# Elementwise work of a hybrid decoder layer divided anew between ScalarE and VectorE

## The chip, the core and the metric

The kernel runs on one core of a Trainium2 chip. The metric is the device time of one execution in microseconds (us). The kernel before takes 871.72 us, the median of three runs (871.52 to 871.88). A profile of one execution shows, per instruction, when it ran on TensorE (PE, its weight loads apart as PEld), VectorE (DVE), ScalarE (ACT), GpSimd (POOL) and in the DMA queues of SyncE (SP).

## The reference

One layer: x is RMS-normed and multiplied with w_in (2048 rows) into the inputs of three groups. Their outputs, each times a SiLU gate, are joined, multiplied with w_out, added to x, and normed again. SEQ is 512, D_MODEL 2048, everything float32.

```python
h = rmsnorm(x, norm_g[l]);  proj = h @ w_in[l]
u = cv_a * jax.nn.sigmoid(cv_b)
u = causal_depthwise_conv(u, conv_w[l], conv_b[l])            # 31 taps, 512 channels
u = jax.nn.silu(layernorm(u, conv_ln_g[l], conv_ln_b[l]))
y_conv = (u @ w_conv_pw[l]) * jax.nn.silu(cv_gate)
logf = jax.nn.log_sigmoid(f_logit + b_f[l])                   # forgetting attention, 8 heads of 128
s = einsum(q, k) * Dh ** -0.5;  s = where(mask, s + c[t] - c[s], -inf);  p = softmax(s)
y_fox = (p @ v) * jax.nn.silu(fox_gate)
mk, mv = split(rmsnorm(mem, mem_norm_g[l]) @ w_mem_kv[l])     # 256 memory tokens, 4 heads
y_mem = memory_attention(mq, mk, mv) * jax.nn.silu(mem_gate)
x = x + concatenate([y_conv, y_fox, y_mem]) @ w_out[l];  return rmsnorm(x, final_g)
```

## The kernel before

Every float32 operand of a product is cut into two rounded parts, hi + lo: ScalarE casts the hi part (line 93, or line 96 with a scale), VectorE subtracts it from the source for the lo part (line 94, or 97). Three products, hi by hi, lo by hi and hi by lo, add up in one PSUM bank (lines 104 to 106 where it is plain, line 732 in the heads, line 981 in the output). Weights come as raw tiles of 128 x 1024 by DMA (six buffers), and become `whi` and `wlo`, which have three buffers each: the cast of a tile waits until TensorE is through with the tile three before it. Of PSUM, five banks circulate under the tag `pj` and three under `at`.

The stages follow each other in time: memory values and keys (to about 62 us; line 104 with the names `mh`, `ml`); x rows (line 212 multiplies each of four 128 x 2048 tiles by its 1/rms, in place) and their transposes by TensorE into `pj` and `at` banks, from which ScalarE makes `hh` and VectorE `hl` (`x_column`, line 262; some columns' transposes run between the products of the last memory key, `pj_689` in the orders below); the first projections by `hh` and `hl` from 66 us; the convolution's inputs with 31 taps each on VectorE and the memory attention; the gates; from about 343 to 690 us the eight forgetting heads; then the output product to 860.8 us, and an end of 8.0 us without TensorE.

A head's two features (queries with keys, values with gate) are made by Winograd's form of Strassen's seven products (`pair`, line 713). Its first product goes to the bank x1, is copied by ScalarE into SBUF as p1 (line 707) and added by VectorE to the third product's bank x2 (line 700). The softmax (`probs`) takes four query blocks of 128, 256, 384 and 512 keys: logits plus bias (line 803), negated maximum (line 805), Exp with a sum (line 807), reciprocal (line 808) and division (line 809). `gate_values` (line 777) makes SiLU from Sigmoid on ScalarE and a product on VectorE. Sigmoid and Exp need different activation tables, so table loads stand on ScalarE.

What an engine runs next is set at build time: the scheduler plans a timeline with its own costs and lays down one fixed order for each engine. An engine waits at the first instruction that isn't ready, whatever is ready behind it. So a change of the elementwise work can change the order of everything near it.

Of the kernel before, what the change touches and what calls it, by code (L numbers as in the profile page):

```python
# [47 lines left out]
def hybrid_layer_kernel(  # L48
# [41 lines left out]
    def split(hi, lo, src, scale=None):  # L90
        """hi + lo == src (times scale): twelve significant bits each."""
        if scale is None:
            ins = nc.scalar.copy(hi, src)  # L93
            nc.vector.tensor_tensor(lo, src, hi.bitcast(F32), ALU.subtract)  # L94
        else:
            ins = nc.scalar.activation(hi, src, AF.Identity, scale=scale)
            nc.vector.scalar_tensor_tensor(
                lo, src, scale, hi.bitcast(F32), ALU.mult, ALU.subtract
            )
        return ins.ins  # L100
# [16 lines left out]
    def operand(src, out=None):  # L117
        """src [P, n, c], whole -> its two parts."""
        if out is None:
            out = tuple(  # L120
                wp.tile(list(src.shape), F32R, tag=t, name=nm(t), bufs=3) for t in ("whi", "wlo")
            )
        split(*out, src)
        return out

    def weights(src, n, c, raw=None, hold=None):
        """src [n * P, c] -> k -> (hi, lo) of its k-th P rows."""
        half = n // 2
        src = src.rearrange("(k p) f -> p k f", p=P)
        parts = []  # L130
        for j in range(2):
            rows = slice(j * half, (j + 1) * half)
            r = raw_tile(half, c) if raw is None else raw[:, rows, :]
            nc.sync.dma_start(out=r, in_=src[:, rows, :])
            parts.append(operand(r, tuple(t[:, rows, :] for t in hold) if hold else None))
        return lambda k: tuple(t[:, k % half, :] for t in parts[k // half])

# [1 line left out]
    ident = const.tile([P, P], F32, name="ident")  # L139
# [11 lines left out]
    ht = ctx.enter_context(tc.tile_pool(name="ht", bufs=1, side="right", reuse_waits="tile"))  # L151
    # x normed, [feature, token], two features' tiles in each
    hs_ = [
# [10 lines left out]

    # ---- start: memory values and keys (rows transposed as they come, their
    # norm applied to the results), x normed and transposed ----
    with tc.tile_pool(name="start", bufs=1) as st:
# [40 lines left out]
        def norm_x(t):  # L208
            rs = st.tile([P, 1], F32, tag="rs", name=nm("rs"), bufs=4)
            sum_squares(rs, xrows[t])  # L210
            rstd(rs)
            nc.vector.tensor_scalar(xrows[t], xrows[t], rs, None, ALU.mult)

# [83 lines left out]
    def project(f0, per=0):  # L297
        """[P features from f0, tokens] in PSUM."""
        w = weights(w_in[:, f0 : f0 + P], KT, P)
# [6 lines left out]
    def silu_of(pool, o, tag, bufs):  # L306
        """silu of a PSUM tile."""
        sg = pool.tile([P, S], F32, tag=tag, name=nm(tag), bufs=bufs)
        nc.scalar.activation(sg, o, AF.Sigmoid)
        nc.vector.tensor_tensor(sg, o, sg, ALU.mult)  # L310
        return sg

# [1 line left out]
    NC = CW // P  # L314
    PAD = TAPS - 1
    with tc.tile_pool(name="conv", bufs=1, reuse_waits="tile") as cp:
# [3 lines left out]
        def taps_of(c, up):  # L320
            a = acc[c]

            def first():
                nc.vector.tensor_scalar(
                    a, up[:, 0:S], cwt[:, c, 0:1], conv_b_c(c), ALU.mult, ALU.add
                )
# [26 lines left out]
        def mem_probs(ma, h, q):  # L353
            qh, ql = q
            pr = []
            for i2 in range(2):
# [15 lines left out]
                for j in range(2):  # L372
                    nc.vector.tensor_scalar(pp[:, j, :], pp[:, j, :], sm[:, j : j + 1], None, ALU.mult)
                pr.append(pp)
# [77 lines left out]
        def forget_columns():  # L452
            c = fgs["c"]
            pc = at((P, NT * NH))
            for i in range(NT):
                nc.tensor.transpose(
                    pc[:, i * NH : (i + 1) * NH], c[:, i * P : (i + 1) * P], ident[:NH, :NH]
                )
            nc.vector.tensor_copy(ccol.rearrange("p i h -> p (i h)"), pc)
        conv_in(0)  # L460
# [7 lines left out]
        with tc.tile_pool(name="matt", bufs=1, reuse_waits="tile") as ma:  # L468
            # the channel norm's sums and the gates run between the heads
            gates = []  # L470
# [26 lines left out]
            def normalise():  # L497
# [15 lines left out]
                for c in range(NC):  # L513
                    a = acc[c]
                    sg = spare()
                    nc.scalar.activation(sg, a, AF.Sigmoid, bias=ln_b_c(c), scale=ln_g_c(c))
                    nc.vector.tensor_scalar(a, a, ln_g_c(c), ln_b_c(c), ALU.mult, ALU.add)
                    nc.vector.tensor_tensor(a, a, sg, ALU.mult)
                    split(*cs[c], a)
# [17 lines left out]

        # sums of h's quarters (token halves by feature halves); the last takes
        # the place of the quarter that no product needs
        spool = ctx.enter_context(  # L540
# [55 lines left out]

    # ---- the output projection's operands; what they need of the room of h and
    # its sums falls free with the last pair's products. The convolution's and
    # the memory's parts of y are multiplied as they are; the heads' parts by the
    # same form as the pairs, with sums of their quarters (token halves by halves  # L600
    # of the heads) ----
    NB = D // S
# [55 lines left out]
    def head_ys(j, fa, fb):  # L658
        """Heads j and 4 + j, whole: their quarters' parts and those of the
        sums, which take the room of fa and fb."""  # L660
        base = [room_h(w, j, (2, S)) for w in "hl"]
# [23 lines left out]

# [1 line left out]
    with tc.tile_pool(name="fox", bufs=1, reuse_waits="tile") as fx:  # L687
# [22 lines left out]
        def pair(fa, fb):  # L710
            """Features fa.. and fb.., P each, by Winograd's form of Strassen's
            seven products: the first in PSUM, by token halves, the second in
            SBUF. In three steps, for another pair's to come between."""
            HK = KT // 2
# [8 lines left out]

            # Sums are taken in PSUM: a product adds onto what its bank holds,
            # which copies and an addition have read or changed before. Only a
            # bank's first product starts afresh.
            def product(o, w, a, start=False):
# [12 lines left out]
            yield  # L740
            p1 = kept(x1, "p1")
            less(b11, b12, b11)
            product(zo, b11, s1, start=True)
            p5 = kept(zo, "p5")
            less(b11, b22, b11)
            product(x2, b11, s2, start=True)
            plus(x2, x2, p1)
            u2 = kept(x2, "u2")
# [18 lines left out]
        def queries_keys(xs, col):  # L767
            q, k = parts("fq"), parts("fk")
            split(*k, col)
            for x_, hi, lo in zip(xs, halves(q[0]), halves(q[1])):  # L770
                split(hi, lo, x_)
            return q, k

        def gate_values(xs, col):
            gate = fx.tile([P, S], F32, tag="fgate", name=nm("fgate"), bufs=2)
            for x_, g in zip(xs, halves(gate)):
                nc.scalar.activation(g, x_, AF.Sigmoid)
                nc.vector.tensor_tensor(g, x_, g, ALU.mult)
            vp = at()
# [7 lines left out]
        def probs(h, q, k):  # L787
# [3 lines left out]
            for i in range(NT):  # L791
                n = (i + 1) * P
                sl = slice(i * P, n)
                b = fx.tile([P, n], F32, tag=f"b{i}", name=nm("b"))
                nc.scalar.activation(b, cb[:, :n], AF.Identity, scale=-1.0, bias=ccol[:, i, h : h + 1])  # L795
                nc.gpsimd.affine_select(  # L796
                    out=b[:, sl], in_=b[:, sl], pattern=[[-1, P]], compare_op=ALU.is_ge,
                    fill=MASKED, base=0, channel_multiplier=1,
                )
                w = max(n, M)  # L800
                sp = at((P, w))
                mm3(sp, (q[0][:, sl], q[1][:, sl]), (k[0][:, :w], k[1][:, :w]), True, True)
                nc.vector.scalar_tensor_tensor(b, sp[:, :n], SC, b, ALU.mult, ALU.add)
                ng = fx.tile([P, 1], F32, tag="ng", name=nm("ng"), bufs=4)
                nc.vector.tensor_reduce(ng, b, AX.X, ALU.max, negate=True)
                sm = fx.tile([P, 1], F32, tag="sm", name=nm("sm"), bufs=4)
                nc.scalar.activation(b, b, AF.Exp, bias=ng, accum_out=sm)
                nc.vector.reciprocal(sm, sm)
                nc.vector.tensor_scalar(b, b, sm, None, ALU.mult)
                res.append(b)  # L810
# [76 lines left out]

# [1 line left out]
    head_ys(3, heads[6], last_y)  # L889
    with tc.tile_pool(name="outp", bufs=1, reuse_waits="tile") as op:  # L890
# [3 lines left out]
        gb = op.tile([P, D], F32, name="gb")  # L894
        # by token halves and column blocks
        res = [[op.tile([P, 2, S], F32, name=f"res{h}{n}") for n in range(NB)] for h in range(2)]
# [22 lines left out]
        def sides(n):  # L919
            """y's other parts; the last time, a token tile at a time and to the end."""  # L920
            final = n == NB - 1
# [19 lines left out]
            for t in range(NT):  # L941
                if not final:
                    add(of(t, n), os_[t])
                    continue
                # the very last one by halves, for less to follow its products
                spans = [ALL] if t < NT - 1 else [slice(0, M), slice(M, S)]
# [133 lines left out]
```

## Time and profile before

| | |
|---|---|
| median of three runs | 871.72 us (871.52 to 871.88) |
| span of the profiled execution | 868.8 us, 14045 instructions |
| around the span | 2.9 us (871.72 less 868.8; the page has no other time of that execution) |
| TensorE busy | 855.3 us, 98% |
| VectorE busy | 704.8 us, 81% |
| ScalarE busy | 436.2 us, 50% |
| chain that ended last | PE 95%, ACT, DVE, DMA and issue 1% each |

The chain is followed back from the last instruction to whatever released each step; it says that TensorE's own work makes up the span, and that there is little waiting to remove. In the timeline view a row has its start, its duration, engine, line, operation, output and inputs (without buffer numbers), its count where several are joined, and in brackets the idle time before it with its releaser. Records of matmuls overlap: a product on 256 columns is 0.28 us long, and the next one starts 0.12 us after it.

### The profile page before, as it was taken

What the parts mean: (1) busy time and instruction counts of PE and PEld (TensorE: products, weight loads), DVE (VectorE), ACT (ScalarE), POOL (GpSimd) and SP (SyncE); (2) the same over time, 40 slices, a digit from 0 to 9 for tenths busy, and PEclk for the clock granted to TensorE, in tenths of its full rate; (3) what the DMA queues carried; (4) which work ended last, traced back from release to release, by engine and by line L of the source; (5) the groups of instructions that cost most, each with busy time, mean ns of one, the idle gap of its engine ahead of it and who ended that gap; (6) DMA issues with size and microseconds to landing.
All of it is one profiled execution on the core that took longest, in us unless ns stands there. A gap on an engine that the chain in (4) does not pass through costs nothing.

```text
span 868.8 us, 14045 instructions
## 1 busy us (share of the span) xinstructions
PE 855.3 (98%) x5562; PEld 775.1 (89%) x5562; DVE 704.8 (81%) x1051; ACT 436.2 (50%) x679; POOL 45.1 (5%) x76
## 2 busy tenths in 40 slices
PE   8999999999999999999999999999999999999996
PEld 6897887888888888999999999999999888998995
DVE  4686799999977998998787878878797886876964
ACT  4874322224346544566565555656464852443523
POOL 1011000000000002010101010101010000000001
PEclk9999999999999999999999999999999999999999
DMA  9972233333332333233434243333334627351415
GB/s 323 356 197 76 70 82 105 97 97 89 94 85 85 109 90 117 79 106 109 121 93 127 74 120 101 107 103 91 107 84 146 239 73 267 97 195 49 146 49 194
DMA packets 143265, 107.52 MB, mean 124 GB/s; under 512 B 3892, under 2 KB 126816, under 8 KB 142560
## 3 DMA queue, kind: packets, MB, share of 16 engines
q1 hardware_dynamic: 141696, 102.52, 39.3%
q0 software_dynamic: 1504, 4.11, 1.3%
q8 instruction: 43, 0.70, 0.3%
q14 instruction: 22, 0.18, 0.1%
HBM read 98.46 MB, written 8.14 MB: 123 GB/s over the span
## 4 chain that ended last, share of the span: by engine, by line
PE 95%; issue 1%; ACT 1%; DVE 1%; DMA 1%; SPq 0%; POOL 0%; POOLq 0%; ACTq 0%
PE pj L732 33%; PE pj L104 13%; PE pj L105 13%; PE pj L106 13%; PE pj L981 8%; PE at L104 3%; PE at L105 3%; PE at L106 3%; PE at L820 1%; DMA raw<-in_w_mem_kv_dram 1%; PE pj L409 0%; PE pj L408 0%; PE pj L262 0%; PE at L262 0%; PE at L782 0%
## 5 line engine op out<-in xcount | busy, mean ns | idle before, releaser
L93 ACT CAST whi<-raw 128x1024 fp32r<-128x1024 f32 x205 | 215.1, 1051 | 324.2 <-PE pj L105 110.9
L94 DVE TENSOR_TENSOR wlo<-raw,whi 128x1024 fp32r<-128x1024 f32 x205 | 250.1, 1221 | 87.5 <-ACT whi L93 86.6
L105 PE MATMUL pj<-hl,whi 128*128 128x512 f32 x352 | 139.6, 397 | 0.0
L106 PE MATMUL pj<-hh,wlo 128*128 128x512 f32 x352 | 139.1, 396 | 0.0
L104 PE MATMUL pj<-hh,whi 128*128 128x512 f32 x352 | 138.9, 396 | 0.0
L732 PE MATMUL pj<-hh,wlo 128*128 128x256 f32 x480 | 135.0, 281 | 0.0
L732 PE MATMUL pj<-hl,whi 128*128 128x256 f32 x480 | 134.9, 281 | 0.0
L732 PE MATMUL pj<-hh,whi 128*128 128x256 f32 x480 | 134.8, 281 | 0.0
L703 DVE TENSOR_TENSOR raw<-raw,raw 128x1024 f32<-128x1024 f32 x76 | 92.7, 1220 | 0.5
L732 PEld LDWEIGHTS pj<-hl,whi 128*128 128x128 f32 x480 | 90.4, 188 | 0.1
L732 PEld LDWEIGHTS pj<-hh,whi 128*128 128x128 f32 x480 | 90.5, 188 | 0.0
L732 PEld LDWEIGHTS pj<-hh,wlo 128*128 128x128 f32 x480 | 90.4, 188 | 0.0
L329 DVE SCALAR_TENSOR_TENSOR acc<-up,cwt,acc 128x512 f32<-128x512 f32 x120 | 85.2, 741 | 0.4
L981 PE MATMUL pj<-whi,rh 128*128 128x256 f32 x448 | 80.0, 280 | 0.7 <-DVE sst L1035 0.4
L104 PEld LDWEIGHTS pj<-hh,whi 128*128 128x128 f32 x352 | 66.1, 188 | 15.9 <-PE pj L262 0.2
L106 PEld LDWEIGHTS pj<-hh,wlo 128*128 128x128 f32 x352 | 66.1, 188 | 15.7
L105 PEld LDWEIGHTS pj<-hl,whi 128*128 128x128 f32 x352 | 66.1, 188 | 15.5
L981 PEld LDWEIGHTS pj<-whi,rh 128*128 128x128 f32 x448 | 68.8, 188 | 1.3 <-DVE res L907 1.1
L981 PE MATMUL pj<-wlo,rh 128*128 128x256 f32 x224 | 62.3, 279 | 0.0
L981 PEld LDWEIGHTS pj<-wlo,rh 128*128 128x128 f32 x224 | 42.1, 188 | 0.2
L796 POOL TENSOR_SCALAR_AFFINE_SELECT b<-b 128x128 f32<-128x128 f32 x32 | 21.3, 676 | 265.6 <-ACT b L795 234.0
L732 PE MATMUL pj<-s0h,whi 128*128 128x256 f32 x120 | 34.9, 291 | 0.0
(302 smaller groups left out, 1720.5 us busy)
## 6 DMA issues: line engine op xcount, KB each, us to landing
raw<-in_w_in_dram SPq DMA_DIRECT2D x104, 512.0 KB, 3.6
raw<-in_w_out_dram SPq DMA_DIRECT2D x32, 512.0 KB, 4.5
raw<-in_w_mem_kv_dram SPq DMA_DIRECT2D x12, 512.0 KB, 7.3
xr<-in_x_dram SPq DMA_DIRECT2D x4, 1024.0 KB, 7.8
res<-in_x_dram SPq DMA_DIRECT2D x8, 512.0 KB, 6.8
out_dram<-res SPq DMA_DIRECT2D x16, 256.0 KB, 2.8
rs<-yd SPq DMA_DIRECT2D x15, 256.0 KB, 4.6
mr<-in_mem_dram SPq DMA_DIRECT2D x8, 256.0 KB, 7.2
```

The source lines that it names most:

```text
L93: ins = nc.scalar.copy(hi, src)
L94: nc.vector.tensor_tensor(lo, src, hi.bitcast(F32), ALU.subtract)
L104: nc.tensor.matmul(o, ah, bh, start=start, stop=False)
L105: nc.tensor.matmul(o, ah, bl, start=False, stop=False)
L106: nc.tensor.matmul(o, al, bh, start=False, stop=stop)
L329: return lambda: nc.vector.scalar_tensor_tensor(a, up[:, j : j + S], cwt[:, c, j : j + 1], a, ALU.mult, ALU.add)
L703: nc.vector.tensor_tensor(o, p, q, ALU.subtract)
L732: nc.tensor.matmul(o, p[:, k, :], q, start=start and k == 0 and i == 0, stop=k == HK - 1 and i == 2, skip_group_check=True,)
L796: nc.gpsimd.affine_select(out=b[:, sl], in_=b[:, sl], pattern=[[-1, P]], compare_op=ALU.is_ge, fill=MASKED, base=0, channel_multiplier=1,)
L820: nc.tensor.transpose(tp[:, (i - j) * P : (i - j + 1) * P], pr[i][:, j * P : (j + 1) * P], ident)
L981: nc.tensor.matmul(o[:, m, :], p, q[:, k, :], start=start and k + m + i == 0, stop=k == HK - 1 and i == 2, skip_group_check=True,)
```

## The change

Six things change. The four row norms of x (line 212) go from VectorE to ScalarE. SiLU is one ScalarE activation instead of a Sigmoid and a VectorE product, in the gates and behind the convolution's norm. The first tap of each convolution channel block and the division of the probabilities, of memory and of forgetting heads, go to ScalarE. The logits with their bias and their maximum are taken in one fused VectorE instruction (`tensor_tensor_reduce`, with signs turned and the scale put into the queries' split). Strassen's first product is copied by ScalarE from bank x1 into bank x2, onto which the third product then adds, so p1 and its VectorE addition go.

```diff
--- before
+++ after
@@ -209,7 +209,7 @@
             sum_squares(rs, xrows[t])
             rstd(rs)
-            nc.vector.tensor_scalar(xrows[t], xrows[t], rs, None, ALU.mult)
+            nc.scalar.mul(xrows[t], xrows[t], rs)
         QC = D // 4
@@ -304,13 +304,12 @@
     def silu_of(pool, o, tag, bufs):
         sg = pool.tile([P, S], F32, tag=tag, name=nm(tag), bufs=bufs)
-        nc.scalar.activation(sg, o, AF.Sigmoid)
-        nc.vector.tensor_tensor(sg, o, sg, ALU.mult)
+        nc.scalar.activation(sg, o, AF.Silu)
         return sg
@@ -321,8 +320,8 @@
             a = acc[c]
             def first():
-                nc.vector.tensor_scalar(
-                    a, up[:, 0:S], cwt[:, c, 0:1], conv_b_c(c), ALU.mult, ALU.add
+                nc.scalar.activation(
+                    a, up[:, 0:S], AF.Identity, scale=cwt[:, c, 0:1], bias=conv_b_c(c)
                 )
@@ -370,7 +369,7 @@
                 nc.vector.reciprocal(sm, sm)
                 for j in range(2):
-                    nc.vector.tensor_scalar(pp[:, j, :], pp[:, j, :], sm[:, j : j + 1], None, ALU.mult)
+                    nc.scalar.mul(pp[:, j, :], pp[:, j, :], sm[:, j : j + 1])
                 pr.append(pp)
@@ -456,7 +455,7 @@
                     pc[:, i * NH : (i + 1) * NH], c[:, i * P : (i + 1) * P], ident[:NH, :NH]
                 )
-            nc.vector.tensor_copy(ccol.rearrange("p i h -> p (i h)"), pc)
+            nc.vector.tensor_scalar(ccol.rearrange("p i h -> p (i h)"), pc, -1.0, None, ALU.mult)
         conv_in(0)
@@ -512,10 +511,7 @@
                 for c in range(NC):
                     a = acc[c]
-                    sg = spare()
-                    nc.scalar.activation(sg, a, AF.Sigmoid, bias=ln_b_c(c), scale=ln_g_c(c))
-                    nc.vector.tensor_scalar(a, a, ln_g_c(c), ln_b_c(c), ALU.mult, ALU.add)
-                    nc.vector.tensor_tensor(a, a, sg, ALU.mult)
+                    nc.scalar.activation(a, a, AF.Silu, bias=ln_b_c(c), scale=ln_g_c(c))
                     split(*cs[c], a)
@@ -738,13 +735,12 @@
             product(x1, b11, a11, start=True)
             yield
-            p1 = kept(x1, "p1")
+            nc.scalar.copy(x2, x1)
             less(b11, b12, b11)
...
             p5 = kept(zo, "p5")
             less(b11, b22, b11)
-            product(x2, b11, s2, start=True)
-            plus(x2, x2, p1)
+            product(x2, b11, s2)
             u2 = kept(x2, "u2")
@@ -767,15 +763,15 @@
             split(*k, col)
             for x_, hi, lo in zip(xs, halves(q[0]), halves(q[1])):
-                split(hi, lo, x_)
+                split(hi, lo, x_, scale=-SC)
             return q, k
...
             gate = fx.tile([P, S], F32, tag="fgate", name=nm("fgate"), bufs=2)
             for x_, g in zip(xs, halves(gate)):
-                nc.scalar.activation(g, x_, AF.Sigmoid)
-                nc.vector.tensor_tensor(g, x_, g, ALU.mult)
+                nc.scalar.activation(g, x_, AF.Silu)
             vp = at()
@@ -792,21 +788,22 @@
                 sl = slice(i * P, n)
                 b = fx.tile([P, n], F32, tag=f"b{i}", name=nm("b"))
-                nc.scalar.activation(b, cb[:, :n], AF.Identity, scale=-1.0, bias=ccol[:, i, h : h + 1])
+                nc.scalar.activation(b, cb[:, :n], AF.Identity, bias=ccol[:, i, h : h + 1])
                 nc.gpsimd.affine_select(
                     out=b[:, sl], in_=b[:, sl], pattern=[[-1, P]], compare_op=ALU.is_ge,
-                    fill=MASKED, base=0, channel_multiplier=1,
+                    fill=-MASKED, base=0, channel_multiplier=1,
                 )
...
                 sp = at((P, w))
                 mm3(sp, (q[0][:, sl], q[1][:, sl]), (k[0][:, :w], k[1][:, :w]), True, True)
-                nc.vector.scalar_tensor_tensor(b, sp[:, :n], SC, b, ALU.mult, ALU.add)
                 ng = fx.tile([P, 1], F32, tag="ng", name=nm("ng"), bufs=4)
-                nc.vector.tensor_reduce(ng, b, AX.X, ALU.max, negate=True)
+                nc.vector.tensor_tensor_reduce(
+                    b, sp[:, :n], b, 1.0, -MASKED, ALU.add, ALU.min, accum_out=ng
+                )
                 sm = fx.tile([P, 1], F32, tag="sm", name=nm("sm"), bufs=4)
-                nc.scalar.activation(b, b, AF.Exp, bias=ng, accum_out=sm)
+                nc.scalar.activation(b, b, AF.Exp, bias=ng, scale=-1.0, accum_out=sm)
                 nc.vector.reciprocal(sm, sm)
-                nc.vector.tensor_scalar(b, b, sm, None, ALU.mult)
+                nc.scalar.mul(b, b, sm)
                 res.append(b)
```

The new sources move the order of the engines as well. The names end in a counter of tiles. In the rows, `whi_939` is a half of the weights of the second feature block that `hh` and `hl` meet (`whi_878` and `whi_884` are those of the first), `xr_...` are rows of x, `mk_...` memory keys.

ScalarE where the row norms end and the first `hh` are made, before:

```order
L93 CAST whi_878<-raw_876 128x1024
L93 CAST mk_120<-kt_665 128x256
L93 CAST whi_884<-raw_882 128x1024
L96 ACTIVATE hh_101<-at_693,cols 128x512
L96 ACTIVATE hh_101<-pj_703,cols 128x512
L96 ACTIVATE hh_103<-at_713,cols 128x512
L96 ACTIVATE hh_103<-pj_723,cols 128x512
L96 ACTIVATE hh_105<-at_733,cols 128x512
L96 ACTIVATE hh_105<-pj_743,cols 128x512
L96 ACTIVATE hh_107<-pj_763,cols 128x512
L93 CAST whi_939<-raw_937 128x1024
```

and now:

```order
L93 CAST whi_878<-raw_876 128x1024
L212 ACTIVATE xr_681<-xr_681,rs_683 128x2048
L93 CAST whi_884<-raw_882 128x1024
L93 CAST mk_120<-kt_665 128x256
L93 CAST whi_939<-raw_937 128x1024
L96 ACTIVATE hh_101<-at_693,cols 128x512
L96 ACTIVATE hh_101<-pj_703,cols 128x512
L96 ACTIVATE hh_103<-at_713,cols 128x512
```

The cast of `whi_939` stood behind the seventh `hh` and stands ahead of the first one now; a row norm stands among the casts.

VectorE at the same place, before:

```order
L94 TENSOR_TENSOR wlo_885<-raw_882,whi_884 128x1024
L97 SCALAR_TENSOR_TENSOR hl_102<-at_693,cols,hh_101 128x512
L97 SCALAR_TENSOR_TENSOR hl_102<-pj_703,cols,hh_101 128x512
L97 SCALAR_TENSOR_TENSOR hl_104<-at_713,cols,hh_103 128x512
L97 SCALAR_TENSOR_TENSOR hl_104<-pj_723,cols,hh_103 128x512
L284 TENSOR_TENSOR kt_850<-pj_689,rbc 128x256
L97 SCALAR_TENSOR_TENSOR hl_106<-at_733,cols,hh_105 128x512
L97 SCALAR_TENSOR_TENSOR hl_106<-pj_743,cols,hh_105 128x512
L97 SCALAR_TENSOR_TENSOR hl_108<-pj_763,cols,hh_107 128x512
L94 TENSOR_TENSOR wlo_940<-raw_937,whi_939 128x1024
```

and now:

```order
L94 TENSOR_TENSOR wlo_885<-raw_882,whi_884 128x1024
L94 TENSOR_TENSOR mk_121<-kt_665,mk_120 128x256
L94 TENSOR_TENSOR wlo_940<-raw_937,whi_939 128x1024
L284 TENSOR_TENSOR kt_850<-pj_689,rbc 128x256
L97 SCALAR_TENSOR_TENSOR hl_102<-at_693,cols,hh_101 128x512
L97 SCALAR_TENSOR_TENSOR hl_102<-pj_703,cols,hh_101 128x512
L97 SCALAR_TENSOR_TENSOR hl_104<-at_713,cols,hh_103 128x512
L97 SCALAR_TENSOR_TENSOR hl_104<-pj_723,cols,hh_103 128x512
L97 SCALAR_TENSOR_TENSOR hl_106<-at_733,cols,hh_105 128x512
L97 SCALAR_TENSOR_TENSOR hl_106<-pj_743,cols,hh_105 128x512
L97 SCALAR_TENSOR_TENSOR hl_108<-pj_763,cols,hh_107 128x512
```

`wlo_940`, which needs `whi_939`, and `kt_850`, which needs the last memory key's product `pj_689`, stood behind the seventh and the fourth `hl`; both now stand ahead of the first.

ScalarE at the last head's probabilities, where the output's first operands begin (`whi_7513` before is `whi_7415` now, `whi_7221` is `whi_7125`, `whi_7386` is `whi_7290`), before:

```order
L93 CAST whi_7221<-raw_6958 128x1024
L93 CAST rs_7277<-rs_7275 128x512
L93 CAST whi_7386<-raw_6962 128x1024
L707 COPY u_980_7162<-pj_6966 128x256
L777 ACT_TABLE_LOAD
L777 ACTIVATE fgate_7414<-pj_6964 128x256
L807 ACT_TABLE_LOAD
L807 ACTIVATE b_7067,sm_7079<-b_7067,ng_7077 128x384
L807 ACTIVATE b_7083,sm_7095<-b_7083,ng_7093 128x512
L93 CAST whi_7513<-raw_7253 128x1024
```

and now:

```order
L804 ACTIVATE b_6975,sm_6986<-b_6975,ng_6984 128x384
L93 CAST whi_7125<-raw_6868 128x1024
L703 COPY u_961_7066<-pj_6876 128x256
L93 CAST rs_7181<-rs_7179 128x512
L804 ACTIVATE b_6990,sm_7001<-b_6990,ng_6999 128x512
L806 ACTIVATE b_6975<-b_6975,sm_6986 128x384
L93 CAST whi_7290<-raw_6872 128x1024
L774 ACT_TABLE_LOAD
L774 ACTIVATE fgate_7318<-pj_6874 128x256
L806 ACTIVATE b_6990<-b_6990,sm_7001 128x512
L93 CAST whi_7415<-raw_7157 128x1024
```

One table load is gone, since both last Exps stand ahead of the gate; two divisions (line 806) have come in. TensorE's order changes there too: nine transposes of 128 x 128 (two of `col`, seven of the probabilities) now stand ahead of the first product with `whi_7415`; before, three products with `whi_7513` stood ahead of two transposes of `col` and three of the probabilities.

## Rows read from the trace of the kernel before

**Rows 1.** Page, part 1: busy us, share of span, instructions of each engine.

```profile
PE 855.3 (98%) x5562; PEld 775.1 (89%) x5562; DVE 704.8 (81%) x1051; ACT 436.2 (50%) x679; POOL 45.1 (5%) x76
```

**Rows 2.** What the TensorE queue waited for: us in total, times, longest.

```profile
PE pj L104 <- ACT mh L96: 2.4, 1, 2.4
...
PE pj L104 <- ACT whi L93: 0.6, 1, 0.6
PE pj L981 <- DVE sst L1035: 0.4, 1, 0.4
PE pj L981 <- DVE res L907: 0.3, 1, 0.3
```

**Rows 3.** Timeline of TensorE, 62 to 66 us: start us, us, what, [idle].

```profile
62.69 0.60 PE L262 MATMUL at<-ident,xr 128*128 128x128 f32 x4
63.12 0.60 PE L262 MATMUL pj<-ident,xr 128*128 128x128 f32 x4
...
66.24 0.47 PE L104 MATMUL pj<-hh,whi 128*128 128x512 f32 x1
```

**Rows 4.** Timeline of ScalarE, same stretch.

```profile
58.84 1.05 ACT L93 CAST whi<-raw 128x1024 fp32r<-128x1024 f32 x1 [2.38 <-issue]
59.80 0.68 ACT L96 ACTIVATE hh<-at,cols 128x512 fp32r<-128x512 f32 x1
...
63.80 1.10 ACT L93 CAST whi<-raw 128x1024 fp32r<-128x1024 f32 x1
```

**Rows 5.** Timeline of VectorE, same stretch.

```profile
61.07 0.74 DVE L97 SCALAR_TENSOR_TENSOR hl<-at,cols,hh 128x512 fp32r<-128x512 f32 x1
...
63.70 0.41 DVE L284 TENSOR_TENSOR kt<-pj,rbc 128x256 f32<-128x256 f32 x1
...
64.69 1.40 DVE L97 SCALAR_TENSOR_TENSOR hl<-pj,cols,hh 128x512 fp32r<-128x512 f32 x2
```

**Rows 6.** Windows at the start: length, busy us per engine, clock, DMA.

```profile
4.00:8.00 4.00, 2.44 (x12) 1.53 (x11) 0.17 (x1) 0.45 (x1) 0.65 (x2) 1.00 0.93 297
8.00:12.00 4.00, 2.98 (x8) 2.02 (x9) 3.38 (x5) 3.04 (x7) 0.00 (x0) 0.66 1.05 391
```

**Rows 7.** Groups of instructions: busy us, mean ns of one, idle before.

```profile
L200 ACT ACTIVATE junk<-xr 128x2048 bf16<-128x2048 f32 x4 | 7.7, 1914 | 0.0
...
L778 DVE TENSOR_TENSOR fgate<-pj,fgate 128x256 f32<-128x256 f32 x16 | 6.7, 421 | 2.6 <-ACT fgate L777 2.6
...
L700 DVE TENSOR_TENSOR pj<-pj,p 128x256 f32<-128x256 f32 x15 | 6.4, 427 | 8.3 <-PE pj L732 8.3
...
L212 DVE TENSOR_SCALAR xr<-xr,rs 128x2048 f32<-128x2048 f32 x4 | 5.1, 1283 | 0.8 <-POOL rs L204 0.7
```

**Rows 8.** Lines 805 and 809 alone: ns min/median/max, first and last start.

```profile
L805 DVE TENSOR_REDUCE ng<-b x32: 273/476/677, 367.4 to 679.7; 128x1 f32<-128x128 f32 x8, 128x1 f32<-128x256 f32 x8, 128x1 f32<-128x384 f32 x8, 128x1 f32<-128x512 f32 x8
L809 DVE TENSOR_SCALAR b<-b,sm x32: 277/382/487, 372.9 to 687.6; 128x128 f32<-128x128 f32 x8, 128x256 f32<-128x256 f32 x8, 128x384 f32<-128x384 f32 x8, 128x512 f32<-128x512 f32 x8
```

**Rows 9.** Timeline of TensorE at the end of the heads.

```profile
681.51 0.39 PE L732 MATMUL pj<-s2h,wlo 128*128 128x256 f32 x1 [0.16 <-DVE wlo L94]
...
683.98 0.28 PE L732 MATMUL pj<-s2l,whi 128*128 128x256 f32 x1
684.10 0.28 PE L732 MATMUL pj<-s2h,wlo 128*128 128x256 f32 x1
684.98 0.96 PE L104 MATMUL pj<-whi,rs 128*128 128x512 f32 x3 [0.60 <-ACT whi L93]
```

**Rows 10.** Timeline of ScalarE, same stretch.

```profile
681.28 1.28 ACT L807 ACT_TABLE_LOAD   x1
...
683.90 1.03 ACT L93 CAST whi<-raw 128x1024 fp32r<-128x1024 f32 x1
```

**Rows 11.** Timeline of VectorE in a middle head.

```profile
497.39 1.21 DVE L94 TENSOR_TENSOR wlo<-raw,whi 128x1024 fp32r<-128x1024 f32 x1
```

**Rows 12.** Timeline of TensorE in the same head.

```profile
500.58 0.28 PE L732 MATMUL pj<-s2h,wlo 128*128 128x256 f32 x1
```

## Prediction

> **What bounds the kernel now.** I read the engines' busy times first. TensorE is busy for 98% of the span, VectorE for 81% and ScalarE for 50% [rows 1]. So work that leaves VectorE shortens nothing by itself; it can only take away a wait of TensorE, and what ScalarE takes over costs only where TensorE comes to wait for it. The list of TensorE's waits comes next: beside the start's (2.4 us the longest) it holds single waits of 0.6 us for a cast of weights, and of 0.4 and 0.3 us for sums of the output stage [rows 2]. The heads have none. The whole that can be won is thus a few microseconds, and what is lost depends on the new order of the engines. So I followed the two orders from stage to stage against the timeline of before, and looked for the places where TensorE waits, or where the order puts something late ahead of something needed. I found one of each kind.
>
> **Part 1, the row norms, 59 to 70 us: slower.** The four multiplications leave VectorE at 1283 ns each and come to ScalarE, where the nearest row is the pass over the same 128 x 2048 at 1914 ns [rows 7]. By itself this costs little: ScalarE has idle time there, 2.38 us in one piece ahead of 58.84 [rows 4]. What costs is the order. The cast of `whi_939` needs the buffer of `whi_677`, three tiles before it, and that is read until the last product of `pj_689` has run. Before, that cast stood behind seven `hh` and ran at 63.80, while the `hh` began at 59.80 [rows 4]. Now it stands ahead of all `hh`, and the `hh` wait with it.
>
> When is the buffer free? Before, transposes follow the last product of `pj_689` at 62.69 [rows 3], so its record ends at about 62.69 + 0.16 = 62.85 (records overlap by 0.16: 0.28 long, one every 0.12, as [rows 9] show at 683.98 and 684.10). Seven transposes of the last x row now stand behind that product and not among its products; four take 0.43 us [rows 3], seven 0.76, so it ends at 62.09. `whi_939` runs from there for 1.05 us (as the cast at 58.84) to 63.14. VectorE's new order then has `wlo_940`, `kt_850` and the seven `hl`. Before, the first `hl` started at 61.07 behind a `wlo` whose cast had ended at 59.89 [rows 4, 5], 1.18 us later; now `wlo_940` lets it pass at 64.32, and `kt_850` takes 0.33 more (from 63.70 to 64.69 are one `kt` and one `hl`, and four `hl` from 61.07 to 63.70 make 0.66 each [rows 5]). So the first `hl` starts at 64.65, the seventh at 68.61, and ends 0.74 later at 69.35. Before, the seventh ended at 66.09 and the first product with `hh`, whose bank it frees, started 0.15 later at 66.24 [rows 3, 5]. Now that is 69.50: **+3.26 us**. The transposes left (28, 3.1 us) fit into TensorE's pauses, since each bank that an `hl` frees takes four of them, 0.43 us, in the 0.66 us until the next `hl`. From 66 us on TensorE had no wait for a long time, so nothing gives the 3.3 us back.
>
> Bounds: 2.5 us if TensorE reaches the end of `pj_689` by another seven transposes (0.76 us) earlier, and 4.0 us if it does so as much later. A further cost is TensorE's clock. At the start, after a wait of 2.4 us in one piece [rows 2], it ran at a mean of 0.66 of its 2.4 GHz in the stretch of 4 us that holds the restart, so at 1.2 GHz for a part of it, and at 1.00 in the stretch before [rows 6]; that is 0.34 x 4 = 1.4 us of full speed lost. The new pause could do the same. Between 0 and 1.4 I take 0, since its longest piece, from 62.85 to `kt_850` at 64.65, is 1.8 us, and the rest is broken up by transposes; 1.4 stays for the range.
>
> **Part 2, the end of the heads, 676 to 686 us: faster.** TensorE waits there twice: 0.16 us of idle before 681.51, which is 0.16 + 0.16 = 0.32 with the records' overlap, for a `wlo`, and 684.98 - 684.10 - 0.12 = 0.76 us for the cast `whi_7513`; the restarts are some 0.1 longer each (0.39 against 0.28) [rows 9]. Together 1.3 us. The first is VectorE's backlog: between 676 and 680 us it ran two maxima, two divisions and a Strassen addition ahead of that `wlo`; in the new order divisions and addition are gone and the maxima are in the fused pass. The second is ScalarE's: a table load of 1.28 us at 681.28 and two Exps stood ahead of the cast, which ran at 683.90 and at once [rows 10]. In the new order the load is gone and the Exps stand earlier, and two divisions have come in: at L809's 382 ns times 1914/1283, the ratio of the row norms [rows 7, 8], some 0.57 us each, 1.14 in all. So the cast ends 0.1 to 0.6 us earlier than its 684.93, at 684.3 to 684.8. TensorE, by 0.43 earlier without the first wait, gets nine transposes (0.98 us) before it needs that cast, at about 684.22 - 0.43 + 0.98 = 684.77. So both waits go: **-1.3 us**, with bounds of 0 and -1.3.
>
> **The other parts, at no cost.** In the heads the fused pass takes the place of a logit pass and a maximum; no row shows such a pass. At the least it saves nothing, at the most the whole maximum (476 ns at the median, 32 times [rows 8]); I take most of it, as one reading of the data falls away. The division leaves VectorE (382 ns at the median, 32 times [rows 8]), as do the gate's product (421 ns, 16 times) and the Strassen addition (427 ns, 15 times) [rows 7]: per head some 1.5 + 0.8 + 0.4 and up to 1.9 us. ScalarE gets 4 x 0.57 = 2.3 us per head. Neither is waited for there today, and the copy between banks follows its product at once, so VectorE's gain is worth 0, and ScalarE's load 0 as long as the casts keep their lead (the last rival). Silu takes the place of Sigmoid, one activation for one. First taps and memory divisions lie in stages without waits of TensorE. In the output stage all the orders but one swap are the same, so its two waits [rows 2] stay; bounds are -1.2, if both go (0.4 + 0.3, and 0.16 of overlap and 0.1 of restart for each, as in part 2), and +0.5.
>
> **The sum.** 868.8 + 3.3 - 1.3 = 870.8 us of span. With the 2.9 us around it (871.72 less 868.8; the profiled execution gives no other time) that is **873.7 us**, 2.0 or 0.23% above 871.72. About 0.2%, 1.74 us, is what a measurement of this kernel can tell from no change.
>
> **Rivals.**
> *The row norm stage costs nothing, or under half.* If the cast of `whi_939` gets its buffer before 60 us, the `hh` start as before, and only part 2 is left: 870.4 to 871.7, no change. For it: ScalarE idles there and VectorE loses 5.1 us of work. Against it: the buffer depends on TensorE, which is late by its own work.
> *Faster: VectorE's relief reaches every wait.* Besides part 2, the output stage's two waits go (1.2 us), as VectorE comes out of the heads ahead, and part 1 doesn't come: 871.72 - 1.3 - 1.2 = 869.2. It decides once part 1 is under 0.7 us. For it: the releasers of both are on VectorE [rows 2]. Against it: the order there is the old one, and the part 1 wait is in the order.
> *Slower still: ScalarE becomes the bound in the heads.* A division waits for a reciprocal on VectorE and holds the casts behind it. The lead is small: a `wlo` ends at 498.60 and is used at 500.58, 1.98 us [rows 11, 12]. At most two divisions stand ahead of a cast, 1.14 us; with a reciprocal that waits for a whole `wlo` (1.21) that is 2.35, or 0.4 us beyond the lead. Over seven heads 2.6 us on top of the forecast: 876.3. It decides as soon as the reciprocal stands behind a `wlo` each time. Against it: ScalarE has idle time in every head, being busy for 50% [rows 1].
> The Trainium skill's page "ScalarE: Activation LUTs" speaks for this rival: its "Rules for kernel authors" say to give `mul` to VectorE and not to ScalarE. The trace agrees on the price of one instruction, 1914 against 1283 ns; by that rule alone the change loses, while the sum above loses by one place in the order.
>
> **How the numbers follow.** Forecast 0.55, stage at no cost 0.25, faster 0.08, ScalarE the bound 0.12. The range goes from 870.6, which takes in most of the no-cost case, to 877.0, which takes in the ScalarE case and the forecast with the clock's 1.4 us (875.1), without part 2 as well (876.4); some 0.15 is left out. The forecast lies close above the bound, so of its 0.55 I give 0.41 to slower and 0.14 to the same; with the ScalarE case slower is 0.53, with the no-cost case same is 0.37, and faster is 0.10.
>
> **What would show it.** Right: in the profile after, the cast ahead of the first `hh` starts at about 62.1 and the first `hh` product at about 69.5; TensorE's waits have none at the end of the heads; the heads repeat at the same pitch. Wrong: a first `hh` product near 66 us, waits on casts within the heads, or a granted clock under 1.00 about 70 us.

## The result and the profile after

The changed kernel takes 872.7 us, the median of 14 runs (872.15 to 873.92), against 871.26 us of the kernel before in 14 runs beside them. The ratio is 1.0019, 95% interval 1.0011 to 1.0026: slower by about 1.65 us. The profiled execution has a span of 870.3 us, 1.5 more than the 868.8 of before. Part 1 of its page:

```profile
PE 855.7 (98%) x5562; PEld 774.9 (89%) x5562; DVE 656.8 (75%) x948; ACT 463.8 (53%) x734; POOL 37.9 (4%) x76
```

VectorE lost 48 us of work and ScalarE gained 28 [rows 1]. TensorE has the same 98%, and what it waits for tells the rest. The longest of its waits after the change (us in total, times, longest):

```profile
PE pj L104 <- ACT mh L96: 2.5, 1, 2.5
PE pj L262 <- DVE kt L284: 1.8, 1, 1.8
...
PE pj L978 <- DVE sst L1032: 0.4, 1, 0.4
PE pj L978 <- DVE res L904: 0.3, 1, 0.3
```

A wait of 1.8 us for `kt` is new. The waits for `whi` (0.6) and `wlo` at the end of the heads are gone, and the two of the output stage are as they were [rows 2].

**The row norms.** TensorE, ScalarE and VectorE at the place of [rows 3 to 5], timelines after the change:

```profile
61.39 0.28 PE L105 MATMUL pj<-ml,whi 128*128 128x256 f32 x1
61.51 0.28 PE L106 MATMUL pj<-mh,wlo 128*128 128x256 f32 x1
...
62.18 0.38 PE L262 MATMUL pj<-ident,xr 128*128 128x128 f32 x2
64.41 0.66 PE L262 MATMUL pj<-ident,xr 128*128 128x128 f32 x4 [1.85 <-DVE kt L284]
...
69.02 0.50 PE L104 MATMUL pj<-hh,whi 128*128 128x512 f32 x1
```

```profile
58.02 2.00 ACT L212 ACTIVATE xr<-xr,rs 128x2048 f32<-128x2048 f32 x1
...
61.71 1.05 ACT L93 CAST whi<-raw 128x1024 fp32r<-128x1024 f32 x1 [0.45 <-PE pj L105]
62.66 0.68 ACT L96 ACTIVATE hh<-at,cols 128x512 fp32r<-128x512 f32 x1
```

```profile
62.79 1.23 DVE L94 TENSOR_TENSOR wlo<-raw,whi 128x1024 fp32r<-128x1024 f32 x1 [0.25 <-ACT whi L93]
63.94 0.42 DVE L284 TENSOR_TENSOR kt<-pj,rbc 128x256 f32<-128x256 f32 x1
64.27 0.74 DVE L97 SCALAR_TENSOR_TENSOR hl<-at,cols,hh 128x512 fp32r<-128x512 f32 x1
```

The last row norm, now on ScalarE, runs from 58.02 to 60.02. The cast of `whi_939` starts at 61.71, right behind the last product that reads its buffer (line 105 at 61.39, through at 61.67; the last product of `pj_689`, at 61.51, reads `wlo` and not `whi`). The `hh` follow at 62.66 and not at 59.80, the first `hl` at 64.27 and not at 61.07. TensorE stands from 62.56 to 64.41, then takes four transposes per `hl`, and comes to the first product with `hh` at 69.02 instead of 66.24. Its clock in two stretches there (length, busy us of PE, PEld, DVE, ACT, POOL, then clock, DMA share, GB/s) does not fall, and the next products with `hh` and `hl` bear that out, starting at 69.35, 69.59 and 69.82, as far apart as before (66.54, 66.78, 67.01):

```profile
62.00:64.00 2.00, 0.56 (x6) 0.32 (x3) 1.75 (x4) 2.00 (x4) 0.00 (x0) 1.00 0.97 247
64.00:66.00 2.00, 1.59 (x11) 1.12 (x11) 2.00 (x5) 2.00 (x4) 0.00 (x0) 1.00 1.00 262
```

The profiled executions differ at the start, where no edit of any run changes an instruction, so the stretches are compared from a mark: TensorE's first 128 x 256 product of the memory keys, at 33.34 us before and 33.05 after. The same subtraction was made for every run below.

| profiled execution | mark | mark to first `hh` product | that product to the end |
|---|---|---|---|
| before | 33.34 | 32.90 | 802.56 |
| after | 33.05 | 35.97 (+3.07) | 801.28 (-1.28) |
| norm_back | 34.50 | 32.90 (0.00) | 801.50 (-1.06) |
| norm_only | 34.12 | 35.98 (+3.08) | 802.80 (+0.24) |
| cast_behind | 33.70 | 34.70 (+1.80) | 801.60 (-0.96) |
| last_back | 34.48 | 33.09 (+0.19) | 801.43 (-1.13) |
| ttr_only | 33.34 | 32.91 (+0.01) | 801.45 (-1.11) |
| nb_two_pass | 32.89 | 32.90 (0.00) | 803.31 (+0.75) |
| nb_div_back | 33.40 | 32.91 (+0.01) | 801.49 (-1.07) |
| act_load3 | 33.20 | 32.92 (+0.02) | 801.58 (-0.98) |

The last column can be read to about 0.25 us and no closer: norm_only changes no instruction of that stretch, and it reads +0.24 there.

**The end of the heads.** TensorE, then ScalarE, after the change, at the place of [rows 9, 10]:

```profile
686.57 0.28 PE L729 MATMUL pj<-s2h,wlo 128*128 128x256 f32 x1
686.69 0.38 PE L778 MATMUL at<-ident,col 128*128 128x128 f32 x2
686.91 0.93 PE L817 MATMUL at<-ident,b 128*128 128x128 f32 x7
687.60 1.18 PE L104 MATMUL pj<-whi,rs 128*128 128x512 f32 x4
```

```profile
680.64 0.72 ACT L804 ACTIVATE b<-b,ng 128x512 f32<-128x512 f32 x1
...
682.92 1.28 ACT L774 ACT_TABLE_LOAD   x1
...
685.10 1.04 ACT L93 CAST whi<-raw 128x1024 fp32r<-128x1024 f32 x1
```

No row has an idle time before it: the products end, nine transposes and then the first products with `whi_7415` follow one another. ScalarE's last Exp is at 680.64, ahead of the one table load at 682.92, and the cast is through at 686.14, 1.46 us before TensorE asks for it. Some durations (mean ns of one) that the trace of before could not show:

```profile
L212 ACT ACTIVATE xr<-xr,rs 128x2048 f32<-128x2048 f32 x4 | 8.0, 1999 | 0.0
...
L806 ACT ACTIVATE b<-b,sm 128x512 f32<-128x512 f32 x8 | 5.7, 716 | 0.0
...
L800 DVE CUSTOM_DVE_ANT_0 b<-at,b 128x512 f32<-128x512 f32 x8 | 5.5, 687 | 0.0
```

The fused pass over 512 columns takes 687 ns; the maximum that it also yields took 677 by itself [rows 8], so that whole pass is saved. The row norm takes 1999 ns on ScalarE, 1283 on VectorE [rows 7].

### The profile page after: what moved, and what is told of

It is laid out like the page before. It is cut to its first block, busy times and chain, and to the rows that moved or that the text cites. A ratio compares the mean times of both kernels' runs of the same rounds, so it can differ in the third digit from the quotient of the medians.

```text
span 870.3 us, 13950 instructions
## 1 busy us (share of the span) xinstructions
PE 855.7 (98%) x5562; PEld 774.9 (89%) x5562; DVE 656.8 (75%) x948; ACT 463.8 (53%) x734; POOL 37.9 (4%) x76
## 4 chain that ended last, share of the span: by engine, by line
PE 96%; DVE 1%; issue 1%; DMA 1%; ACT 0%; SPq 0%; POOL 0%; POOLq 0%; ACTq 0%
PE pj L729 34%; PE pj L104 13%; PE pj L105 13%; PE pj L106 13%; PE pj L978 8%; PE at L104 3%; PE at L106 3%; PE at L105 3%; PE at L817 1%; DMA raw<-in_w_mem_kv_dram 1%; PE pj L262 0%; PE at L262 0%; PE pj L407 0%; PE pj L408 0%; PE at L778 0%
## 5 line engine op out<-in xcount | busy, mean ns | idle before, releaser
L106 PEld LDWEIGHTS pj<-hh,wlo 128*128 128x128 f32 x352 | 66.1, 188 | 15.7
L729 PE MATMUL pj<-s0l,whi 128*128 128x256 f32 x120 | 34.4, 286 | 0.0
```

The costliest lines, as they stand in the source:

```text
L106: nc.tensor.matmul(o, al, bh, start=False, stop=stop)
L729: nc.tensor.matmul(o, p[:, k, :], q, start=start and k == 0 and i == 0, stop=k == HK - 1 and i == 2, skip_group_check=True,)
```

## The experiments

All were timed beside the kernel before, whose median was 871.05 us for norm_back, norm_only, cast_behind and ttr_only, and 870.81 us for the four others.

**norm_back**: the row norms back on VectorE, all else changed.

```diff
-            nc.scalar.mul(xrows[t], xrows[t], rs)
+            nc.vector.tensor_scalar(xrows[t], xrows[t], rs, None, ALU.mult)
```

> The changed kernel with the four row norms of x on VectorE as before; all else of the change stays. Theory (the row norm's place costs, the end of the heads gains): the first product with hh comes near 66 us again instead of 69.0, the end of the heads has no wait, so about 872.7 - 2.9 = 869.8 us, 1.4 under the kernel before (ratio 0.9984). Rival (ScalarE's other new work costs time in the heads, and hides a part of it): the time stays at or above 871.3, ratio 1.000 or more.

Measured: 870.03 us, ratio 0.9985 (0.9976 to 0.9994). The mark and the first product with `hh`:

```profile
34.50 0.39 PE L104 MATMUL pj<-mh,whi 128*128 128x256 f32 x1
...
67.40 0.48 PE L104 MATMUL pj<-hh,whi 128*128 128x512 f32 x1
```

That product stands 32.90 us behind the mark, as before, and the gain of the rest of the change is left (-1.06 us for -1.28, within the 0.25). This version beats both kernels, the one before by 0.15%.

**norm_only**: the same line the other way round, in the kernel before.

```diff
-            nc.vector.tensor_scalar(xrows[t], xrows[t], rs, None, ALU.mult)
+            nc.scalar.mul(xrows[t], xrows[t], rs)
```

> The kernel before with the four row norms on ScalarE and nothing else changed. Theory: the cast of the next weights again stands ahead of all hh on ScalarE, TensorE waits some 1.8 us for kt and the first product with hh comes near 69 us; the waits at the end of the heads stay; 871.3 + 2.9 = 874.2 us, ratio 1.0033. Rival (the row norms cost nothing by themselves and only shift with the rest of the change): 871.3, ratio 1.000.

Measured: 874.76 us, ratio 1.0042 (1.0029 to 1.0054), and TensorE's waits:

```profile
PE pj L262 <- DVE kt L284: 1.8, 1, 1.8
...
PE pj L104 <- ACT whi L93: 0.6, 1, 0.6
...
PE pj L732 <- DVE wlo L94: 0.2, 1, 0.2
```

The wait for `kt` is the one of the changed kernel, the cost by the table is 3.08 us, and the two waits at the end of the heads are still there. So the two places don't touch one another, and their sum (+3.07 - 1.28 = +1.79 us) is the change. The ratio is somewhat above the expected 1.0033, which lies in its interval.

**cast_behind**: the changed kernel, with ScalarE's casts of the second feature block's weights held behind the seventh `hh` (an order between two instructions, no wait for data).

```diff
-            ob = project(C_B + c * P, 6)
+            ob = project(C_B + c * P, 6, made[7] if c == 0 else None)
...
+            with tc.issue_after(behind):
+                w = weights(w_in[:, f0 : f0 + P], KT, P)
```

> The changed kernel, row norms on ScalarE, but the cast of the weights that need the busy buffer is put behind the seventh hh, as it stood before. Theory (mostly the order): hh start at about 61.2 instead of 62.7, hl at about 62.5, the seventh hl ends near 67.5, and the first product with hh comes at 67.6 instead of 69.0; what is left is ScalarE's last row norm at 58.0 to 59.9, which puts off a cast and the memory key behind it. 872.7 - 1.4 = 871.3, ratio to before 1.000. Rival 1 (only the order costs): 66.2 and 869.8, ratio 0.9984. Rival 2 (ScalarE's added 7.6 us cost, the order nothing): 69.0 and 872.7, ratio 1.0018.

Measured: 871.79 us, ratio 1.0008 (0.9999 to 1.0017). By the table the first product with `hh` comes 1.80 us later than before; in the changed kernel it was 3.07. So 1.27 us came back, where 1.4 were expected. ScalarE, TensorE and VectorE:

```profile
58.67 2.00 ACT L212 ACTIVATE xr<-xr,rs 128x2048 f32<-128x2048 f32 x1
60.58 1.03 ACT L93 CAST whi<-raw 128x1024 fp32r<-128x1024 f32 x1
...
62.59 0.69 ACT L96 ACTIVATE hh<-at,cols 128x512 fp32r<-128x512 f32 x1 [0.68 <-PE at L264]
```

```profile
62.16 0.28 PE L106 MATMUL pj<-mh,wlo 128*128 128x256 f32 x1
62.28 0.27 PE L264 MATMUL at<-ident,xr 128*128 128x128 f32 x1
```

```profile
61.64 1.23 DVE L94 TENSOR_TENSOR wlo<-raw,whi 128x1024 fp32r<-128x1024 f32 x1 [1.43 <-ACT whi L93]
62.78 0.42 DVE L94 TENSOR_TENSOR mk<-kt,mk 128x256 fp32r<-128x256 f32 x1
63.31 0.75 DVE L97 SCALAR_TENSOR_TENSOR hl<-at,cols,hh 128x512 fp32r<-128x512 f32 x1
```

The `hh` stand ahead of that cast now, and yet the first `hl` starts only at 63.31. Two ways lead to it, and both are late by the last row norm. One goes by TensorE: the transposes of the last x row have left their place among the memory key's products and start at 62.28, behind the last of them (62.16), although the row norm is through at 60.67. ScalarE is idle for 0.68 us until a transpose lets it make the first `hh`, which ends at 63.28. The other goes by ScalarE and VectorE, and is the one that was expected: the row norm puts off the cast at 60.58, the `wlo` waits 1.43 us for it, a part of a memory key stands behind that, and VectorE comes to the `hl` at about 63.11 (a pass over 256 columns lets the next one start after 0.33 us). So the transposes end last, by some 0.2 us, and without their delay about 1.6 of the 1.80 us would stay; no run separates the two. That cast's place in the order makes 1.27 us of the 3.07, and the late row norm the other 1.80. The size was near the expected one, but "mostly the order" is not borne out; neither rival is.

**last_back**: the changed kernel, with the last of the four row norms on VectorE.

```diff
-            nc.scalar.mul(xrows[t], xrows[t], rs)
+            if t == NT - 1:
+                nc.vector.tensor_scalar(xrows[t], xrows[t], rs, None, ALU.mult)
+            else:
+                nc.scalar.mul(xrows[t], xrows[t], rs)
```

> The changed kernel with the norm of the last x row alone on VectorE; the three others stay on ScalarE. Theory (only the last row's norm costs, by being late: its seven transposes fall behind the memory key's product, and the cast of the next weights comes ahead of the hh): the transposes stand among the product's matmuls again, hh start at about 60.2 us, the first product with hh within 0.5 us of the kernel before; 871.1 - 1.3 + 0.3 = 870.1, ratio 0.999. Rival (each of the four costs a share of the 3.1 us, as ScalarE's time): three quarters stay, 870.0 + 2.3 = 872.3, ratio 1.0014.

Measured: 869.67 us, ratio 0.9988 (0.9979 to 0.9997). ScalarE goes from its casts to the `hh` without an idle:

```profile
60.42 0.40 ACT L93 CAST mk<-kt 128x256 fp32r<-128x256 f32 x1
60.73 0.68 ACT L96 ACTIVATE hh<-at,cols 128x512 fp32r<-128x512 f32 x1
```

Three row norms on ScalarE, 6 us of work, cost 0.19 us by the table. The fourth one's place on ScalarE is the cause of the other 2.88; the rival of equal shares is out. Taking it back cures the late transposes and the late casts together, so this run does not tell the one from the other.

**ttr_only**: the kernel before with the fused pass alone (with the signs and the scale that belong to it).

```diff
-                nc.vector.scalar_tensor_tensor(b, sp[:, :n], SC, b, ALU.mult, ALU.add)
-                nc.vector.tensor_reduce(ng, b, AX.X, ALU.max, negate=True)
+                nc.vector.tensor_tensor_reduce(
+                    b, sp[:, :n], b, 1.0, -MASKED, ALU.add, ALU.min, accum_out=ng
+                )
...
```

> The kernel before with the fused pass for logits and maximum alone (signs and scale with it); divisions, SiLU and Strassen's first copy stay on VectorE. Theory: the fused pass alone takes both waits away at the end of the heads, since both last Exps come ahead of the gate and a table load goes: 871.3 - 1.3 = 870.0, ratio 0.9985. Rival (the relief of VectorE by divisions and addition is needed for the wait of 0.32 us, the fused pass takes the 0.76 alone): 870.4, ratio 0.999. Rival (the divisions on ScalarE move the Exps): 871.3, ratio 1.000.

Measured: 869.92 us, ratio 0.9988 (0.9979 to 0.9996), and -1.11 us of the -1.28 by the table, all of it within the 0.25. The interval also holds the first rival's 0.999, but TensorE's waits have neither the one for `whi` nor the one for a `wlo` any more. ScalarE at the end of the heads:

```profile
677.90 0.71 ACT L808 ACTIVATE b<-b,ng 128x512 f32<-128x512 f32 x1
...
679.93 1.28 ACT L777 ACT_TABLE_LOAD   x1
...
681.50 1.05 ACT L93 CAST whi<-raw 128x1024 fp32r<-128x1024 f32 x1
```

With the maximum there earlier, the last Exp (677.90) runs ahead of the gate, one table load is left (679.93), and the cast comes at 681.50. Neither divisions nor SiLU nor Strassen's copy were needed.

**nb_two_pass**: norm_back, with the fused pass taken apart into two.

```diff
-                nc.vector.tensor_tensor_reduce(
-                    b, sp[:, :n], b, 1.0, -MASKED, ALU.add, ALU.min, accum_out=ng
-                )
+                nc.vector.tensor_tensor(b, sp[:, :n], b, ALU.add)
+                nc.vector.tensor_reduce(ng, b, AX.X, ALU.min)
```

> The changed kernel with the row norms on VectorE (870.0 us), and the fused pass taken apart again: an addition of logits and bias and a minimum behind it, two VectorE passes. All else of the change stays. Theory (the fused pass alone clears the end of the heads): both waits of TensorE come back in the main, with the second table load ahead of the cast: 0.8 to 1.3 us more, 870.8 to 871.3, ratio 0.9997 to 1.000. Rival (the divisions and the SiLU do a part): at most 0.3 us more, 870.3, ratio 0.999.

Measured: 871.49 us, ratio 1.0005 (0.9996 to 1.0014), 1.8 us by the table over norm_back, more than the 0.8 to 1.3 expected. ScalarE, and the wait of TensorE:

```profile
680.18 1.28 ACT L774 ACT_TABLE_LOAD   x1
...
681.88 1.28 ACT L803 ACT_TABLE_LOAD   x1
...
683.90 1.03 ACT L93 CAST whi<-raw 128x1024 fp32r<-128x1024 f32 x1
```

```profile
PE pj L104 <- ACT whi L93: 1.4, 1, 1.4
```

The maximum is late again, the order has the gate between the last two Exps, there are two table loads, and the cast follows at 683.90. So the gain hangs on the fused pass, but not as two waits that come back: the one for the cast is longer than before the change (1.4 for 0.6), and the one of 0.32 us for a `wlo` stays away, so that one goes with VectorE's other relief as well; which part of it does it was not tried.

**nb_div_back**: norm_back, with the heads' divisions on VectorE.

```diff
-                nc.scalar.mul(b, b, sm)
+                nc.vector.tensor_scalar(b, b, sm, None, ALU.mult)
```

> The changed kernel with the row norms on VectorE (870.0 us), and the division of the forgetting probabilities back on VectorE too. Theory (neither engine is waited for in the heads): 870.0, ratio 0.9985, no wait of TensorE in the heads or at their end. Rival (a multiplication belongs on VectorE, ScalarE's 2.3 us per head cost something): under 869.5, ratio 0.998. Rival (VectorE's relief counts): over 870.5, ratio 0.9995.

Measured: 869.81 us, ratio 0.9988 (0.9980 to 0.9997), like norm_back. The interval alone reaches the ratios of both rivals; the stretches decide, which differ by 0.01 us from norm_back's, and TensorE has no wait in the heads. Which of the two engines divides makes no difference here.

**act_load3**: norm_back, with three more multiplications behind each division, whose results nobody reads.

```diff
                 nc.scalar.mul(b, b, sm)
+                spare_t = fx.tile([P, S], BF16, tag="spare", name=nm("spare"))
+                nc.scalar.mul(spare_t[:, :n], b, sm)
+                nc.scalar.mul(spare_t[:, :n], b, sm)
+                nc.scalar.mul(spare_t[:, :n], b, sm)
```

> The changed kernel with the row norms on VectorE (870.0 us), and each division in the heads followed by three more multiplications of the same size on ScalarE into a tile that nobody reads: some 6.6 us more of ScalarE in each head of 45. Theory (ScalarE's idle time holds it, the casts keep a lead): no wait of TensorE in the middle heads, at most 1 us more in all, 870 to 871. Rival (ScalarE is close to being the bound, since a cast leads its product by some 2 us): a wait of 0.5 us or more in each head, 874 us or more, ratio 1.003.

Measured: 870.16 us, ratio 0.9990 (0.9981 to 0.9999). One head's length of norm_back, and of act_load3 with all the waits of its TensorE:

```profile
428.00:473.16 45.16, 45.16 (x376) 44.89 (x375) 33.84 (x47) 28.32 (x48) 2.18 (x5) 1.00 0.39 107
```

```profile
428.00:473.16 45.16, 45.16 (x376) 44.90 (x376) 33.76 (x48) 34.06 (x61) 2.58 (x5) 1.00 0.40 106
```

```profile
PE pj L104 <- ACT mh L96: 2.4, 1, 2.4
PE at L177 <- POOL ident masks.py:199: 1.4, 1, 1.4
PE pj L982 <- DVE sst L1036: 0.4, 1, 0.4
PE pj L982 <- DVE res L908: 0.2, 1, 0.2
```

ScalarE goes from 28.3 to 34.1 us of 45.2 (5.7 more, where 6.6 were expected), and TensorE has work in all of them in both. So ScalarE is far from being the bound in the heads.

## Why the prediction was right, step by step

**The bound** was read rightly: with TensorE at 98%, 48 us less on VectorE moved nothing except where TensorE waited, at two places.

**Part 1** came at 3.07 us for 3.26, and its steps at their times when the 0.29 us of the earlier mark are added: end of `pj_689` 62.08 (forecast 62.09), first `hl` 64.56 (64.65), first product 69.31 (69.50). The buffer of the cast comes free with the product of line 105 and not with the last one, which makes 0.09 of the 0.19 us that are missing. The longest pause was 1.85 us (forecast 1.8), and the clock stayed at 1.00, as taken; that was a choice by two pauses, and why this one leaves the clock alone was not tried. But the step "by itself this costs little" was wrong. The cast did hold the `hh`, in the order given; cast_behind shows that with the cast out of the way the row norm still costs 1.80 us, by the late transposes and by the casts that it puts off. The prediction has the transposes only as seven that let the product end sooner, and the put-off casts not at all. By its working cast_behind should have brought back the whole 3.07; it brought 1.27. The sum did not suffer, since of several ways to the first `hl` the longest decides.

**Part 2** came at -1.28 us for -1.3, with no wait left; as the same stretch gives -0.96 to -1.13 in the other kernels with the fused pass and no wait at the end of the heads, a fit to the last tenths is luck. Its reasons were half right: the table load and the early Exps are what frees the cast, and ttr_only shows that the fused pass brings these about. The divisions and the addition that were named for the 0.32 us aren't needed where the fused pass is. The lead of the cast was underrated: 1.46 us, where the working had it about even.

**The other parts** were worth nothing, as said: nb_div_back and act_load3 show it for the heads, and the output stage kept both its waits. The fused pass saved the whole maximum, the upper end of its bounds.

**The sum.** 3.07 - 1.28 = 1.79 us from the mark, 1.65 by the ratio, for 2.0 in the forecast. That is 0.19%, at the border that the chances were drawn at, with 0.2% for what can be told; the interval of the ratio excludes no change. The time itself was forecast 1.0 us too long, 873.7 for 872.7, above all by the 2.9 us around the span: that was a median less the span of another execution, and the 14 runs after have 1.72 to 1.85 (872.15 less 870.3 in the profiled one).

**The rivals.** The row norm stage did cost (norm_only). VectorE's relief did not reach the output stage. ScalarE as the bound in the heads is out by act_load3: a lead of 1.98 us for one cast is no measure of the room. That the new order moves the added work to where ScalarE idles is likely, but was not followed in the trace. The rule of the Trainium skill that gives `mul` to VectorE ("ScalarE: Activation LUTs", "Rules for kernel authors") agrees with the durations, 1999 against 1283 ns for a row norm and 716 against at most 487 for a division over 512 columns [rows 7, 8]. It decided nothing: 32 divisions and three of four row norms on ScalarE cost 0.2 us at the most, and the fourth cost 2.9 by where it stood.

## What to carry to other kernels

Where one engine is busy for 98%, a change on the others is read from its few waits, and from what the new order puts ahead of the instructions on which it waits next; shares of busy time say little. When a wait is explained, ask what would end last if it went: here a second one, 1.80 of 3.07 us, lay right under the first, and a third within 0.2 us of that. A gain and a loss at different places can be kept apart: the row norms back on VectorE, or the last one alone, turn +0.19% into -0.15% or -0.12%.

## What the runs showed of the hardware

The start differs by up to 1.6 us from one profiled execution to another (mark at 32.89 to 34.50 us in the table), about as much as the whole change costs, though no edit changes an instruction there. After the first wait for `mh`, TensorE runs at 1.2 GHz for a while: windows of 8 to 12 and 12 to 16 us show a granted clock of 0.66 and 0.92 before, 0.57 and 1.00 after, 0.55 and 0.60 in norm_back, whose mark is the latest. In norm_only they read 1.00 although its products of 512 columns start every 0.43 us there until 14 us (12.25, 12.68, 13.11, 13.53) and every 0.23 us after 15.7, so the reading is not complete. So spans of single profiles are compared from a mark behind the start, or by medians of many runs.

A fused pass with an addition and a minimum over 512 columns takes 687 ns, hardly more than the addition alone in nb_two_pass:

```profile
L800 DVE TENSOR_TENSOR b<-at,b 128x512 f32<-128x512 f32 x8 | 5.5, 681 | 0.0
```

Some 0.08 us to read the result come on top, but in the changed kernel the next instruction of VectorE starts together with that read (both at 679.24 at the end of the heads).
